# Summing the adaLN vectors of a two-layer backbone on VectorE in place of TensorE

## The chip, the cores and the metric

One core of one Trainium2 chip. The metric is the device time of the whole kernel in microseconds, the median of the runs. TensorE (PE) multiplies, VectorE (DVE) and ScalarE (ACT) do elementwise work, GpSimd (POOL) and SyncE (SP) issue the loads here.

## What is computed

Two streams of 256 tokens, 1024 wide each (context and latent), pass through two layers. Layer 0 mixes with an S5 scan beside four retention heads, layer 1 with mLSTM heads; a squared-ReLU MLP follows each. Before every mixer and every MLP stands an RMS norm with an adaLN shift and scale, and behind every one an adaLN gate. The adaLN vectors are products of two conditioning vectors with a wide weight:

```python
silu_c = jax.nn.silu(c)          # latent stream
silu_cc = jax.nn.silu(c_ctx)     # context stream
for layer in range(DEPTH):       # DEPTH = 2, N_MOD = 6, mod_w[layer] is 1024 x 6144
    ctx_out = layer < DEPTH - 1
    m_lat = [m[:, None, :] for m in jnp.split(silu_c @ mod_w[layer] + mod_b[layer], N_MOD, axis=-1)]
    m_ctx = jnp.split(silu_cc @ mod_w[layer] + mod_b[layer], N_MOD, axis=-1)
    h_lat = modulate(rms_norm(lat, norm_mix_g[layer]), m_lat[0], m_lat[1])
    h_ctx = modulate(rms_norm(cx, norm_mix_g[layer]), m_ctx[0], m_ctx[1])
    ...                          # the mixer of the layer
    lat = lat + m_lat[2] * y_lat
    h2 = modulate(rms_norm(lat, norm_mlp_g[layer]), m_lat[3], m_lat[4])
    lat = lat + m_lat[5] * sq_relu_mlp(h2, mlp_w1[layer], mlp_w2[layer])
    if ctx_out:                  # layer 0 alone: the context stream gets the same
        ...
return rms_norm(lat, final_norm_g)
```

So layer 0 needs all six vectors (c = 0 to 5) for both streams; layer 1 needs c = 0 and 1 for both streams and c = 2 to 5 for the latent stream alone.

## The kernel before, in words

Activations lie with the model width on the partitions (eight tiles of 128 x 512: 256 context tokens, then 256 latent tokens). Every large product is made of three reduced-precision products: the weight tile (128 x 1024) and the activation are each split into a high and a low part, the high part by a cast on ScalarE, the low part by a subtraction on VectorE. A matmul of 128 x 512 with such a part is the common TensorE instruction; each weight tile thus asks for one `CAST w` on ScalarE and one `TENSOR_TENSOR w` on VectorE before its products can be finished.

*Order of the work.* Nothing is written out in order. `body`, `even_mixer`, `mlp` and `odd_mixer` only record operations, each under the name of a group (`chu11` a part of the S5 scan, `head1` two retention heads, `glu`, `wo0` the output projection of layer 0, `nm0` the norm before layer 0's MLP, `mlp00a` the first half of that MLP, `nm` and `gt` the norm and first products of layer 1's mixer). `Plan.order` then places them on five in-order queues (PE, V, A, G for GpSimd, SP) with a list scheduler: its costs, capacities `CAPS` and, for each group, a pair of numbers in `SHIFT` and `AGAIN` (how far the group's due time is moved, and how far ahead it may take a buffer). All instructions are issued in one loop in `Plan.emit`, so each carries one line number, L693 before and L698 after.

*The vectors.* `sc` holds SiLU of both conditioning vectors (columns 0 and 1 of 32; the other 30 are zero). The first two vectors of layer 0 go through `mod_first`, loaded by SP. The other ten go through `mod(l, c, both)`: eight rows of the weight (tiles of 128 x 1024 from `in_modc`, loaded by GpSimd into the buffers `m`, of which there are 2, or `e`, of which there are 5 and which the scan uses too). With `both` (layer 0's c = 2 to 5 and layer 1's c = 0, 1) TensorE adds up each row as it lands, four products of 32 columns side by side (`ps<-m,sc` or `ps<-e,sc`). Without it (layer 1's c = 2 to 5, latent alone) VectorE sums the rows into a tile `e`, scaled per partition (`SCALAR_TENSOR_TENSOR e<-e,sc,e`, the first of eight a `TENSOR_SCALAR`), and TensorE then makes four products of 32 columns with the constant `second` (a column of ones at place 1), which add over the partitions. Either way ScalarE copies the result to `mrow`, TensorE transposes it and VectorE adds the bias into `mc`. For the norm `mod_gain` makes `gm` of it.

*Who needs them when.* Layer 0's c = 2 is read by the residual additions of `wo0`, c = 3 and 4 by `nm0`, c = 5 by the residual additions of the MLP. The norm `nm0` sums squares with products by `ones`, computes the reciprocal root on VectorE in tiles `rs`, spreads it by products with `ident`, and then scales, shifts and splits tile by tile.

Of the kernel before, what the change touches and what calls it, by code (L numbers as in the profile page):

```python
# [21 lines left out]
HORIZON, ROUNDS = 92, 6  # L22
SHIFT = {"": (-41, -100), "chu00": (-8, 8), "chu01": (0, 5), "chu10": (-1, -89), "chu11": (2, 27), "decay0": (-1, 46),
# [16 lines left out]
AGAIN = (  # L40
# [654 lines left out]
def body(tc, I, out, dbg=None):  # L695
    nc = tc.nc
    plan = Plan(CAPS)
# [3 lines left out]
    def const(shape, tag, dt=F32):  # L701
        return plan.buf("@" + tag, shape, dt)
# [64 lines left out]
    gm = [[const((128, 8, 2), f"gm{l}{j}") for j in range(2)] for l in range(2)]  # L767
    sc = const((128, 8, 32), "sc")
    msel = const((128, 2), "msel")
    second = const((128, 32), "second")  # L770

    def stage(src):
        st = wt()
# [1040 lines left out]
```

## Time and profile before

| | |
|---|---|
| median of 3 runs | 1227.14 us (1225.52 to 1228.25) |
| profiled execution | 1225.47 us, its span 1223.7 us |
| granted TensorE clock, mean | 0.978 |
| TensorE, VectorE, ScalarE busy | 96%, 63%, 45% of the span |

A row of the busy time by stage gives the stretch, its length, then busy us and number of instructions (x) for PE, PE's weight load, DVE, ACT and POOL, where they have any, then the granted clock, the share of the DMA engines and GB/s. A row of the timeline gives start, busy time, engine, line, operation, what it writes and reads (numbers of buffers left out), and in brackets how long the engine sat idle before it and what ended that. A row of the chain gives start, length and what it was.

### The profile page before, as it was taken

How to read it: one execution, taken by the hardware profiler on the slowest of the kernel's cores; microseconds unless marked ns; L12 is line 12 of the kernel's file. 1: busy time of each engine (PE TensorE's matmuls, PEld its weight loads, DVE VectorE, ACT ScalarE, POOL GpSimd, SP SyncE). 2: the span in 40 equal slices, each digit the busy share in tenths (PEclk: the TensorE clock that was granted, in tenths of full speed). 3: DMA queues.
4: the chain of work that ended last, by engine and by line, in shares of the span. 5: the costliest groups of instructions: out<-in, count | busy, mean ns of one | idle time of the engine just before them, and what ended most of it. 6: DMA issues, size and time to landing. Idle time of an engine off the chain costs nothing.

```text
span 1223.7 us, 17752 instructions
## 1 busy us (share of the span) xinstructions
PE 1172.9 (96%) x6968; PEld 972.0 (79%) x6968; DVE 770.6 (63%) x1535; ACT 552.8 (45%) x890; POOL 43.2 (4%) x85
## 2 busy tenths in 40 slices
PE   5799999999989999999999999999999998999996
PEld 3577877777758888888787877767888897999996
DVE  8999899464454347434346485956577566765655
ACT  3635535552343332223243146676665444643542
POOL 0001001101020001000000000000000000000000
PEclk9799999999999999999999989999999998999998
DMA  9764225446472337523253532202222253455552
GB/s 353 260 205 132 89 87 160 162 136 226 159 269 95 121 102 233 182 87 124 92 188 138 198 121 86 64 24 69 90 75 87 87 178 136 169 172 190 207 190 70
DMA packets 61923, 177.75 MB, mean 145 GB/s; under 512 B 10768, under 2 KB 17104, under 8 KB 61840
## 3 DMA queue, kind: packets, MB, share of 16 engines
q1 hardware_dynamic: 50320, 134.67, 33.0%
q0 software_dynamic: 11520, 41.95, 10.0%
q8 instruction: 55, 0.90, 0.3%
q14 instruction: 28, 0.23, 0.1%
HBM read 174.01 MB, written 2.59 MB: 144 GB/s over the span
## 4 chain that ended last, share of the span: by engine, by line
PE 64%; issue 16%; DVE 13%; DMA 3%; ACT 3%; POOL 0%; SPq 0%; DVEq 0%; POOLq 0%; ACTq 0%
PE ps L693 64%; DVE b L693 10%; DMA e<-in_modc 2%; DVE w L693 2%; ACT b L693 2%; ACT w L693 1%; DMA dram<-b 1%; DVE e L693 1%; DVE rs L693 0%; DMA vec<-in_vec 0%; ACT L693 0%; DVE sm L693 0%; POOL e L693 0%; DVE pw L693 0%; DVE lgs L693 0%
## 5 line engine op out<-in xcount | busy, mean ns | idle before, releaser
L693 PE MATMUL ps<-b,w 128*128 128x512 f32 (+1 forms) x4920 | 921.3, 346 | 7.6 <-ACT w L693 4.0
L693 PEld LDWEIGHTS ps<-b,w 128*128 128x128 f32 x4920 | 769.6, 190 | 133.8 <-issue 8.8
L693 DVE TENSOR_TENSOR w<-w,w 128x1024 fp32r<-128x1024 f32 x209 | 255.6, 1223 | 225.1 <-PE ps L693 173.5
L693 ACT CAST w<-w 128x1024 fp32r<-128x1024 f32 x209 | 218.5, 1048 | 374.2 <-PE ps L693 165.3
L693 DVE TENSOR_TENSOR b<-b,b 128x512 f32<-128x512 f32 (+4 forms) x276 | 153.1, 574 | 66.8 <-ACT b L693 57.8
L693 PE MATMUL ps<-b,b 128*128 128x256 f32 (+5 forms) x832 | 149.1, 333 | 1.8 <-DMA b<-dram 1.5
L693 PEld LDWEIGHTS ps<-b,b 128*128 128x128 f32 (+1 forms) x832 | 110.9, 183 | 27.1 <-issue 18.2
L693 ACT COPY b<-ps 128x256 f32<-128x256 f32 (+4 forms) x132 | 58.5, 459 | 42.4 <-PE ps L693 30.8
L693 ACT ACTIVATE b<-ps 128x256 f32<-128x256 f32 (+1 forms) x112 | 49.8, 459 | 50.7 <-PE ps L693 48.9
L693 ACT CAST b<-b 128x512 fp32r<-128x512 f32 (+2 forms) x112 | 56.5, 527 | 34.5 <-DVE b L693 31.3
L693 ACT ACTIVATE b<-b 128x256 f32<-128x256 f32 (+2 forms) x75 | 37.4, 513 | 47.6 <-DVE b L693 42.1
L693 DVE SCALAR_TENSOR_TENSOR b<-b,vec,b 128x512 f32<-128x512 f32 (+1 forms) x80 | 53.2, 691 | 8.9 <-ACT b L693 8.3
L693 DVE TENSOR_TENSOR b<-b 128x256 f32<-128x256 f32 (+2 forms) x95 | 43.6, 476 | 15.8 <-ACT b L693 15.7
L693 DVE SCALAR_TENSOR_TENSOR b<-ps,mc,b 128x256 f32<-128x256 f32 x72 | 31.8, 478 | 32.8 <-PE ps L693 32.8
L693 ACT ACT_TABLE_LOAD x36 | 46.2, 1283 | 7.5 <-DMA cc<-in_cc 6.8
L693 POOL DMA_DIRECT2D e<-in_modc x56 | 29.8, 533 | 412.5 <-DVE e L693 238.5
L693 DVE SCALAR_TENSOR_TENSOR e<-e,sc,e 128x1024 f32<-128x1024 f32 x28 | 35.9, 1281 | 5.6 <-DMA e<-in_modc 5.3
L693 DVE SCALAR_TENSOR_TENSOR b<-ps,b 128x512 f32<-128x512 f32 (+1 forms) x32 | 19.3, 620 | 25.2 <-PE ps L693 16.7
L693 PE MATMUL ps<-e,sc 128*32 128x256 f32 x240 | 20.7, 444 | 10.6 <-DVE sc L693 8.6
L693 PEld LDWEIGHTS ps<-w,b 128*128 128x128 f32 x192 | 24.1, 188 | 3.1 <-issue 2.1
L693 PE MATMUL ps<-w,b 128*128 128x256 f32 x192 | 26.1, 287 | 0.0
L693 DVE TENSOR_TENSOR b<-pw,b 128x512 f32<-128x512 f32 x36 | 23.9, 681 | 0.0
(120 smaller groups left out, 525.6 us busy)
## 6 DMA issues: line engine op xcount, KB each, us to landing
w<-in_w SPq DMA_DIRECT2D x128, 512.0 KB, 4.4
e<-in_modc POOLq DMA_DIRECT2D x56, 512.0 KB, 5.1
m<-in_modc POOLq DMA_DIRECT2D x24, 512.0 KB, 4.8
w<-in_evin SPq DMA_DIRECT2D x16, 512.0 KB, 4.5
w<-in_mlx SPq DMA_DIRECT2D x16, 512.0 KB, 3.8
w<-in_mlo SPq DMA_DIRECT2D x16, 512.0 KB, 3.7
w<-in_mlout SPq DMA_DIRECT2D x16, 512.0 KB, 4.1
b<-in_xT SPq DMA_DIRECT2D x16, 256.0 KB, 8.3
```

The source lines that it names most:

```text
L693: o.ins.append(getattr(engine, name)(*[f(a) for a in args], **{k: f(v) for k, v in kw.items()}))
```

## The change

`mod` no longer sums rows on TensorE for any vector. VectorE sums the rows for each stream that is needed, into one tile `e` per stream (two for c = 2 to 5 of layer 0 and c = 0, 1 of layer 1), and TensorE then makes four products of 32 columns per stream with the constant `pick`, whose part s has ones in column s; both streams' products add into one bank. Each vector has a group of its own (`mod02` to `mod15`). The table of offsets is another one, with another `HORIZON`.

```diff
-HORIZON, ROUNDS = 92, 6
+HORIZON, ROUNDS = 70.0, 6
...
-    second = const((128, 32), "second")
+    pick = const((128, 2, 32), "pick")
...
         pr = ps()
-        tag = "m" if (l, c) < (0, 5) else "e"
-        with plan.group(f"mod{l}{'pe' if both else 'dve'}"):
-            acc = None if both else wt(tag="e")
+        streams = (0, 1) if both else (1,)
+        with plan.group(f"mod{l}{c}"):
+            acc = {s: wt(tag="e") for s in streams}
             for k in range(8):
-                st = wt(tag=tag)
+                st = wt(tag="m" if (l, c) < (0, 5) else "e")
                 with plan.group(plan.name + ".s"):
                     G.dma_start(st, I["modc"][6 * l + c - 2, k])
-                if both:
-                    for q in range(4):
-                        PE.matmul(pr[32 * q:32 * q + 32, 0:256], sc[:, k, :], st[:, 256 * q:256 * q + 256], start=k == 0, stop=k == 7)
-                elif k == 0:
-                    ts(acc, st, sc[:, k, 1:2], MUL)
-                else:
-                    stt(acc, st, sc[:, k, 1:2], acc, MUL, ADD)
-            if not both:
+                for s in streams:
+                    if k == 0:
+                        ts(acc[s], st, sc[:, k, s:s + 1], MUL)
+                    else:
+                        stt(acc[s], st, sc[:, k, s:s + 1], acc[s], MUL, ADD)
+            for s in streams:
                 for q in range(4):
-                    PE.matmul(pr[32 * q:32 * q + 32, 0:256], second, acc[:, 256 * q:256 * q + 256], start=True, stop=True)
+                    PE.matmul(pr[32 * q:32 * q + 32, 0:256], pick[:, s], acc[s][:, 256 * q:256 * q + 256],
+                              start=s == streams[0], stop=s == 1)
...
-    V.memset(x.second, 0.0)
-    V.memset(x.second[:, 1:2], 1.0)
+    V.memset(x.pick, 0.0)
+    for s in range(2):
+        V.memset(x.pick[:, s, s:s + 1], 1.0)
```

What the new order does is seen at two places. In its rows a buffer's name carries two numbers, the second its place in the order of making. The first place is TensorE's queue between the last product of `wo0` and the first of `mlp00a`. Before (its last twelve rows; `rs` is the reciprocal root, `mrow` a vector on its way into `mc`, the last two rows are the MLP's):

```order
L693 MATMUL ps_702_3314<-e_703_3320,sc_65 32x256 x4
L693 MATMUL ps_453_1989<-m_705_3333,sc_65 32x256 x4
L693 MATMUL ps_702_3314<-e_707_3347,sc_65 32x256 x4
L693 MATMUL ps_716_3399<-ident_73,rs_713_3377 128x128 x4
L693 MATMUL ps_453_1989<-m_708_3352,sc_65 32x256 x4
L693 MATMUL ps_702_3314<-e_711_3369,sc_65 32x256 x4
L693 MATMUL ps_453_1989<-ident_73,mrow_719_3416 128x128 x2
L693 MATMUL ps_702_3314<-e_712_3371,sc_65 32x256 x4
L693 MATMUL ps_702_3314<-e_714_3381,sc_65 32x256 x4
L693 MATMUL ps_702_3314<-e_715_3392,sc_65 32x256 x4
L693 MATMUL ps_732_3462<-b_727_3449,w_679_3177 128x512
L693 MATMUL ps_732_3462<-b_727_3449,w_681_3197 128x512
```

And now, from `wo0`'s last product:

```order
L698 MATMUL ps_646_2933<-b_641_2909,w_662_3062 128x512
L698 MATMUL ps_691_3229<-ones_97,b_658_3045 128x1
L698 MATMUL ps_691_3229<-ones_97,b_666_3083 128x1
L698 MATMUL ps_691_3229<-ones_97,b_658_3045 128x1
L698 MATMUL ps_691_3229<-ones_97,b_666_3083 128x1
L698 MATMUL ps_691_3229<-ones_97,b_658_3045 128x1
L698 MATMUL ps_691_3229<-ones_97,b_666_3083 128x1
L698 MATMUL ps_691_3229<-ones_97,b_658_3045 128x1
L698 MATMUL ps_691_3229<-ones_97,b_666_3083 128x1
L698 MATMUL ps_693_3248<-ident_155,rs_692_3238 128x128 x4
L698 MATMUL ps_700_3269<-b_695_3256,w_673_3130 128x512
L698 MATMUL ps_700_3269<-b_695_3256,w_676_3154 128x512
```

The steps with `sc` are gone from there, and only the norm's own products stand between projection and MLP.

The second place is VectorE's queue where the GLU ends and `wo0` begins. Before (rows with `vec` are the GLU's, `w` are low parts of weights, rows with `mc` are `wo0`'s residual additions with c = 2):

```order
L693 SCALAR_TENSOR_TENSOR b_640_2957<-ps_628_2906,vec_77,b_629_2914 128x8x64
L693 TENSOR_TENSOR b_644_2977<-b_640_2957,b_642_2965 128x512
L693 TENSOR_TENSOR w_658_3044<-w_619_2866,w_630_2925 128x1024
L693 TENSOR_TENSOR w_659_3046<-w_622_2872,w_638_2953 128x1024
L693 SCALAR_TENSOR_TENSOR b_645_2979<-ps_652_2993,mc_56_255,b_645_2979 128x256 x2
L693 TENSOR_TENSOR w_664_3082<-w_631_2927,w_661_3053 128x1024
```

And now (the sums of c = 4, one row of the weight for both streams each two lines):

```order
L698 SCALAR_TENSOR_TENSOR e_543_2480<-m_627_2851,sc_89,e_543_2480 128x1024
L698 SCALAR_TENSOR_TENSOR e_580_2643<-m_627_2851,sc_89,e_580_2643 128x1024
L698 SCALAR_TENSOR_TENSOR e_543_2480<-m_644_2921,sc_89,e_543_2480 128x1024
L698 SCALAR_TENSOR_TENSOR e_580_2643<-m_644_2921,sc_89,e_580_2643 128x1024
L698 SCALAR_TENSOR_TENSOR e_543_2480<-m_647_2941,sc_89,e_543_2480 128x1024
L698 SCALAR_TENSOR_TENSOR e_580_2643<-m_647_2941,sc_89,e_580_2643 128x1024
L698 SCALAR_TENSOR_TENSOR e_543_2480<-m_649_2960,sc_89,e_543_2480 128x1024
L698 SCALAR_TENSOR_TENSOR e_580_2643<-m_649_2960,sc_89,e_580_2643 128x1024
L698 SCALAR_TENSOR_TENSOR e_543_2480<-m_650_2978,sc_89,e_543_2480 128x1024
L698 SCALAR_TENSOR_TENSOR e_580_2643<-m_650_2978,sc_89,e_580_2643 128x1024
L698 TENSOR_TENSOR w_652_3010<-w_626_2841,w_640_2904 128x1024
L698 TENSOR_TENSOR w_654_3021<-w_502_2329,w_559_2545 128x1024
```

Ten sums have come in ahead of the two weight splits that stood there. In all, the 48 sums of c = 2, 3 and 4 have come onto VectorE ahead of `nm0`, beside the same other work as before. The sums of c = 3 and 4 of layer 1 have moved from before the norm `nm` to behind it, into layer 1's mixer.

More of the change, by code (lines that the diff above doesn't have):

```diff
@@ L21 @@
 CAPS = {"b": 59, "w": 10, "e": 5, "m": 2, "ps": 8, "mrow": 2, "rs": 3, "tz": 2, "mv": 2, "mv1": 2, "den": 2}
-HORIZON, ROUNDS = 92, 6
-SHIFT = {"": (-41, -100), "chu00": (-8, 8), "chu01": (0, 5), "chu10": (-1, -89), "chu11": (2, 27), "decay0": (-1, 46),
[16 rows of a table removed]
-AGAIN = (
[20 rows of a table removed]
+HORIZON, ROUNDS = 70.0, 6
+SHIFT = {"": (-36, 109), "chu00": (-51, 3), "chu01": (0, 156), "chu10": (0, -53), "chu11": (2, 27), "decay": (1, -71),
[19 rows of a table added]
+AGAIN = (
[5 rows of a table added]
+         (25.8, 220), "gat1.w": (99.4, 400), "glu": (-13.5, -16), "glu.w": (0, 280), "gt": (-16.2, 106), "gt.w":
[16 rows of a table added]
 )
@@ L821, in mod @@
                 PE.transpose(pr[:, 256 + 128 * j:384 + 128 * j], row[:, 128 * j:128 * j + 128], ident)
-            s0 = 0 if both else 1
+            s0 = streams[0]
             b = vc("modb", 48 * l + 8 * c, 8).rearrange("p (q j) -> p q j", j=2)
```

76 rows, old and new, of tables (AGAIN, SHIFT) are left out of this document.

## The prediction

> **What bounds the kernel now.** I read the page first (busy shares and the forty slices), then busy time by stage, then the chain of waits, and at the places it names the timeline. On the page, these rows show who is busy when; a slice is 30.6 us.
>
> ```profile
> PE 1172.9 (96%) x6968; PEld 972.0 (79%) x6968; DVE 770.6 (63%) x1535; ACT 552.8 (45%) x890; POOL 43.2 (4%) x85
> ...
> PE   5799999999989999999999999999999998999996
> DVE  8999899464454347434346485956577566765655
> ...
> PEclk9799999999999999999999989999999998999998
> ```
>
> TensorE looks busy throughout, but VectorE is full in the first seven slices. The busy time by stage (busy us and instructions of PE, weight load, DVE, ACT, POOL; then clock and DMA) separates the two:
>
> ```profile
> 0.00:210.00 210.00, 183.85 (x1263) 144.00 (x1264) 195.46 (x542) 100.25 (x192) 12.37 (x27) 0.95 0.54 185
> 10.00:210.00 200.00, 182.77 (x1255) 143.80 (x1256) 191.23 (x510) 97.11 (x187) 10.90 (x21) 0.95 0.53 182
> 120.00:150.00 30.00, 28.92 (x222) 23.98 (x222) 24.37 (x70) 15.92 (x32) 0.53 (x1) 0.94 0.37 116
> 210.00:340.00 130.00, 128.56 (x720) 97.42 (x718) 63.61 (x112) 57.18 (x89) 9.16 (x18) 1.00 0.51 171
> 0.00:348.00 348.00, 318.62 (x2056) 244.99 (x2056) 263.03 (x660) 159.38 (x284) 25.75 (x52) 0.97 0.54 182
> 340.00:358.00 18.00, 14.23 (x156) 7.05 (x152) 11.00 (x30) 4.66 (x10) 6.86 (x13) 0.91 0.98 350
> 358.00:720.00 362.00, 362.00 (x1589) 292.27 (x1588) 177.21 (x236) 115.07 (x162) 14.84 (x28) 1.00 0.43 145
> 720.00:778.00 58.00, 53.67 (x233) 41.14 (x232) 40.99 (x89) 38.11 (x61) 0.00 (x0) 0.91 0.14 46
> ```
>
> Until 210 us VectorE sets the pace: after the first 10 us it is busy 191.23 of 200 (95.6%). From 210 to 340 TensorE does (128.56 of 130), with VectorE half idle (63.61). Then comes a hole from 340 to 358, where both wait and the DMA engines are full (0.98). From 358 to 720, layer 0's MLP, TensorE has no idle time at all, so there every TensorE instruction added or removed counts.
>
> The hole, in the chain of waits (first row) and the timeline of all engines (the rest):
>
> ```profile
> 340.41 5.21 DMA e<-in_modc
> ...
> 338.55 0.96 PE L693 MATMUL ps<-b,w 128*128 128x512 f32 x3
> ...
> 345.67 0.64 PE L693 MATMUL ps<-e,sc 128*32 128x256 f32 x8 [0.81 <-DMA e<-in_modc]
> ...
> 348.22 0.16 DVE L693 TENSOR_SCALAR rs<-ps 128x4 f32<-128x4 f32 x1 [3.08 <-PE ps L693]
> ...
> 354.78 0.17 DVE L693 TENSOR_TENSOR mc<-ps,vec 128x16 f32<-128x16 f32 x1
> ...
> 357.60 2.70 PE L693 MATMUL ps<-b,w 128*128 128x512 f32 x10 [0.74 <-ACT b L693]
> ```
>
> The last product of layer 0's output projection ends at 339.5; the MLP's first stands at 357.6, 18.1 us later. Between them TensorE sums adaLN vectors row by row as the rows land, and `mc`, the MLP's scale, is written only at 354.78. The same boundary one layer on, where no vector needed for the norm waits for rows:
>
> ```profile
> 720.22 0.64 PE L693 MATMUL ps<-e,second 128*32 128x256 f32 x8
> ...
> 722.77 0.16 DVE L693 TENSOR_SCALAR rs<-ps 128x4 f32<-128x4 f32 x1
> ...
> 728.25 1.22 PE L693 MATMUL ps<-b,w 128*128 128x512 f32 x2 [1.51 <-ACT b L693]
> ```
>
> It takes 8.0 us from 720.2, of which 5.5 lie behind the first `rs`.
>
> **Part 1: what leaves and enters TensorE.** Six vectors times eight rows are 48 steps of four products (8 instructions in the trace). Busy time of these alone, in four stretches, and of the pair products that four vectors use already:
>
> ```profile
> 0.00:66.00 66.00, 16.48 (x152) 5.14 (x152) 0.45 (x2) 0.22 (x1) 0.87 0.77 286
> 66.00:210.00 144.00, 9.99 (x128) 3.21 (x128) 0.00 (x0) 0.00 (x0) 0.99 0.43 138
> 210.00:340.00 130.00, 7.83 (x112) 2.72 (x112) 0.00 (x0) 0.00 (x0) 1.00 0.51 171
> 340.00:358.00 18.00, 9.71 (x124) 3.05 (x120) 0.00 (x0) 0.00 (x0) 0.91 0.98 350
> 600.00:730.00 130.00, 2.56 (x32) 0.63 (x32) 0.00 (x0) 0.98 0.45 156
> ```
>
> The first row holds 128 instructions of the first two vectors, which stay, so 24/8 = 3 steps go there, 16 before 210, 14 before 340 and 15 in the hole: 48. One step costs 7.83/14 = 0.56 us beside other work. The 19 before 210 lie where VectorE sets the pace: worth nothing. Twelve more products of the kept kind are added: six before the MLP, six after it, in stretches where TensorE is full. The six after cost 6 x 0.56 = 3.4 us (bounds: 6 x 0.64 = 3.8 by the last row, and 0 if they fall into waits). **+3.4.**
>
> **Part 2: what enters VectorE.** Rows of the sums it does today (by tile; the third from the timeline, four in a row):
>
> ```profile
> L693 DVE SCALAR_TENSOR_TENSOR e<-e,sc,e x28: 1273/1282/1286, 465.7 to 714.4; 128x1024 f32<-128x1024 f32 x28
> L693 DVE TENSOR_SCALAR e<-e,sc x4: 746/750/753, 453.9 to 674.7; 128x1024 f32<-128x1024 f32 x4
> 471.35 5.24 DVE L693 SCALAR_TENSOR_TENSOR e<-e,sc,e 128x1024 f32<-128x1024 f32 x4
> ```
>
> One stream of one vector is 0.75 + 7 x 1.28 = 9.7 us, both 19.45. Three vectors (c = 2, 3, 4) have to be there before or at the MLP's norm: +58.4 us. The other three (6 streams, another 58.4) stand in the MLP, where VectorE is busy 177.21 of 362: hidden by TensorE, and if that cover went they would cost their length.
>
> VectorE did 263.0 us up to the norm's first `rs` at 348.2; now 263.0 + 58.4 = 321.4 must be done before the same point, since otherwise the same instructions stand before it. Of these 195.5 are done by 210, leaving 125.9 where 67.6 stood. TensorE up to there falls from 318.6 by 9.99 + 7.83 and some, so VectorE becomes the longer of the two. If it stays as full as from 10 to 210 (95.6%), 125.9 takes 131.7 and `rs` comes at 341.7; the order leaves nothing but the norm itself behind it on TensorE, so the MLP starts 5.5 later: 347.2.
>
> Against that stands the place in VectorE's order where ten sums of c = 4 follow each other (five rows) ahead of two weight splits of the output projection. The rows pass through two tiles `m`, and a tile is refilled only after both its sums:
>
> ```profile
> DMA to landing us min/median/max: 3.7/4.9/12.0
> DMA to landing us min/median/max: 3.8/4.5/7.5
> ```
>
> (The first is all loads of these rows, the second those from 450 to 510, where VectorE did such sums.) Two rows take 2.56 + 4.9 = 7.5, so 3.7 each against 2.56 of work: 1.2 lost per row, 6 for five. TensorE has the GLU's products to do meanwhile, so I take half, 3.0, between 0 and 6. The MLP then starts at 350.2 and not at 357.6: **-7.4.** Bounds of this term: VectorE without any idle time and no row waits, 210 + 125.9 + 5.5 = 341.4 (-16.2); and as full as from 120 to 150, its worst stretch while it set the pace (24.37 of 30, 81%), with 6 of row waits, 210 + 155 + 11.5 = 376.5 (+18.9). I take the first value since it is the mean over 200 us of the same kind of work.
>
> **Part 3: the rest.** The sums of two one-stream vectors (c = 3, 4 of layer 1) move behind layer 1's norm, 19.4 us into a stretch where VectorE is busy 40.99 of 58 and TensorE 53.67: the 17 idle hold one of them, if waits there leave room. Bounds 0 and 9.7 (one vector all in the way); I take 1.0, nearer the idle row. **+1.0.** The row loads are the same 80 on POOL's queue. The first 210 us are written in another order too (more of the scan ahead of the heads); I cost it at nothing as long as VectorE stays as full there as now, and a percent less would cost 2.
>
> Sum: -7.4 + 3.4 + 1.0 = -3.0. The profiled execution took 1225.5 (span 1223.7), which gives 1222.5; the median of the runs lies 1.7 above it, so 1224.
>
> **A rule against it.** `TENSOR_SCALAR` takes 750 ns where the two-operand form takes 1282 for as many elements. The Trainium skill, SBUF — State Buffer, section SBUF: two separate sides, says that a VectorE operation in a two-port mode (which such a faster form points to) locks GpSimd out, so that loads issued by GpSimd starve for descriptors; all 80 row loads are issued there. In the trace, loads beside such sums landed in a median 4.5, no later than all of them at 4.9, which does not bear it out.
>
> **The rivals.**
> - *TensorE stays the bound* (0.17). VectorE's sums all fit into its idle time. Then 14 x 0.56 = 7.8 of steps go and 3.4 of products come between 210 and 340, and the hole shrinks from 18.1 to 8.0: -14.5, with +3.4 and +0 behind it -11: 1216, and less if the 16 steps before 210 (9.99) count too: 1206. For it: 85 us of VectorE idle before 348 (348 - 263). Against: 14.5 of them lie before 210.
> - *VectorE becomes the bound and loses time* (0.27), the case on the other side. It works in order, and between 210 and the norm it must wait for products of the heads, for casts and for rows, while weight splits for TensorE queue behind the sums. The change turns to a loss when the MLP starts after 357.6 - 4.4 = 353.2, so `rs` with 3.0 of row waits by 344.7: 125.9 of 134.7, a share of 93.5%. Below it the kernel is slower; at 87%, half way to the worst stretch, the MLP starts at 363.2: +5.6 + 4.4, 1237; at 81% 1247. For it: no stretch before asked both engines for so much.
> - *The wait only changes its owner* (0.18): rows and sums end as late as TensorE's steps did, MLP at about 354: 1227.
> - *Row loads starve behind VectorE* (0.05), the case of the rule above: at the longest landing seen, 12.0, a row takes (2.56 + 12.0)/2 = 7.3, five rows lose 23.6 in place of 3.0: 1245.
>
> **The numbers.** The forecast has 0.33. About 0.2% (2.5 us) is what a measurement of this kernel can tell from no change. Of the forecast 0.28 is faster by more, with 0.17 from the first rival: 0.45. Same: 0.05 of the forecast and the third rival, 0.23. Slower: 0.27 + 0.05 = 0.32. The forecast's own range is 1218 to 1228; the whole, between the first rival's two values and the second's, with about 0.1 left out at each end, 1208 to 1243.
>
> **What would show it.** Right: the hole before the MLP near 8 us without row steps; first MLP product near 350; VectorE busy over 93% from 210 to there; row waits of some 3 us before the ten sums of c = 4; MLP stretch longer by 3. Wrong: MLP start after 353 with TensorE waiting for `w` splits in the GLU or output projection; a granted clock under 1.00 between 210 and 340; row loads landing later than 6 us; layer 1's mixer longer by over 3.

## The result: slower by 1.0%, and the profile after

The changed kernel takes 1239.43 us (median of 4 runs, 1236.22 to 1241.21) against 1226.33 of the kernel before beside it (1225.47 to 1228.25): a ratio of 1.0102, 95% interval 1.0076 to 1.0127. I had forecast 1224. The profiled execution took 1240.03, its span 1238.2; before it was 1225.47 and 1223.7.

The page after, the rows that were shown of before (a slice is now 31.0 us):

```profile
PE 1162.5 (94%) x6680; PEld 975.0 (79%) x6680; DVE 876.8 (71%) x1632; ACT 552.5 (45%) x887; POOL 43.3 (3%) x85
PE   3899989899979999999999989999999997999996
DVE  8999899899764764666845467986557766755564
PEclk9899899999979999999999989899999998999998
```

TensorE has lost 10 us of work and VectorE has gained 106, as the change says. VectorE's full stretch now reaches to the tenth slice, where it was seven before. The busy time by stage:

```profile
0.00:210.00 210.00, 174.90 (x1184) 145.97 (x1185) 195.34 (x519) 112.18 (x203) 2.52 (x8) 0.94 0.43 147
210.00:340.00 130.00, 122.57 (x560) 92.08 (x559) 113.74 (x178) 47.02 (x77) 12.71 (x24) 0.99 0.50 166
210.00:353.00 143.00, 131.78 (x600) 99.80 (x598) 120.82 (x193) 50.89 (x82) 12.71 (x24) 0.97 0.49 166
345.70:358.30 12.60, 5.64 (x25) 5.32 (x25) 6.33 (x19) 2.63 (x6) 0.00 (x0) 0.59 0.16 60
358.30:724.00 365.70, 365.07 (x1614) 293.62 (x1615) 216.34 (x272) 119.22 (x166) 20.66 (x39) 1.00 0.47 156
724.00:734.50 10.50, 6.52 (x54) 5.22 (x52) 7.24 (x22) 5.12 (x10) 1.06 (x2) 0.80 0.34 120
```

Until 210 us VectorE does what it did (195.34, before 195.46). From 210 to 353, where the norm's first `rs` comes, it works 120.82 of 143, a share of 84%. The hole ahead of layer 0's MLP (345.7 to 358.3) is 12.6 us long with the clock at 0.59.

Cut at TensorE's first product of layer 0's MLP, of layer 1's mixer and of layer 1's MLP, the two traces give:

| stretch | before | after | difference |
|---|---|---|---|
| start to layer 0's MLP | 357.6 | 358.3 | +0.7 |
| layer 0's MLP, to the mixer's first product | 370.6 | 376.2 | +5.6 |
| layer 1's mixer, to its MLP's first product | 298.6 | 306.7 | +8.1 |
| the rest | 196.9 | 197.0 | +0.1 |

So nothing was gained ahead of the MLP, where I had put 7.4, and two stretches that I had put at 3.4 and 1.0 cost 13.7. How exact is one such trace? Up to the end of the output projection the changed kernel and four kernels below (`a_no1314`, `a_back`, `a_back2`, `a_warm`) issue the same instructions; their profiled executions reached it at 345.7, 343.6, 347.2, 346.2 and 343.9. A stage is good to about 2 us on either side, and I read smaller differences only where a row names their cause.

*Ahead of the MLP.* VectorE's waits between 210 and 353 (total, times, longest), one of its row waits, the norm's first row on VectorE, and TensorE's queue around the hole:

```profile
DVE e L698 <- DMA m<-in_modc: 7.6, 7, 3.5
DVE w L698 <- PE ps L698: 4.1, 4, 2.3
DVE rs L698 <- PE ps L698: 3.7, 1, 3.7
DVE b L698 <- ACT b L698: 3.6, 5, 1.2
DVE b L698 <- PE ps L698: 2.0, 1, 2.0
```

```profile
233.90 1.28 DVE L698 SCALAR_TENSOR_TENSOR e<-m,sc,e 128x1024 f32<-128x1024 f32 x1 [3.48 <-DMA m<-in_modc]
352.80 0.16 DVE L698 TENSOR_SCALAR rs<-ps 128x4 f32<-128x4 f32 x1 [3.73 <-PE ps L698]
```

Then TensorE:

```profile
344.71 0.95 PE L698 MATMUL ps<-b,w 128*128 128x512 f32 x3
349.22 3.55 PE L698 MATMUL ps<-ones,b 128*128 128x1 f32 x16 [3.56 <-DVE b L698]
354.69 2.05 PE L698 MATMUL ps<-ident,rs 128*128 128x128 f32 x8 [1.93 <-DVE rs L698]
358.25 8.07 PE L698 MATMUL ps<-b,w 128*128 128x512 f32 x27 [1.51 <-ACT b L698]
```

VectorE waits most for weight rows. From 210 us to the end of the output projection TensorE now waits 7.3 us in all, 1.4 before. The longest of these waits, 3.76 us at 235.8, is for a result of VectorE and stands right behind the row wait shown, so there the wait for a row went on to TensorE. In the hole TensorE first waits 3.56 us for the last residual sum; then 16 products by `ones` take 3.55 us, and those by `ident` 2.05. In the hole of the kernel before, between its row steps, the same products took 1.95 and 1.44:

```profile
346.24 1.95 PE L693 MATMUL ps<-ones,b 128*128 128x1 f32 x16
350.91 1.44 PE L693 MATMUL ps<-ident,rs 128*128 128x128 f32 x8
```

*In the MLP.* TensorE's instructions from the MLP's first product to its last, by form (count, busy us, mean ns, idle time before them), in the kernel before:

```profile
L693 PE MATMUL ps<-b,w 128*128 128x512 f32 x1536 | 358.6, 395 | 0.7 <-ACT b L693 0.7
L693 PE MATMUL ps<-b,b 128*128 128x128 f32 x19 | 2.6, 275 | 0.0
L693 PE MATMUL ps<-e,second 128*32 128x256 f32 x16 | 1.3, 391 | 0.0
```

And after:

```profile
L698 PE MATMUL ps<-b,w 128*128 128x512 f32 x1536 | 360.3, 396 | 2.1 <-ACT b L698 1.5 <-DVE w L698 0.6
L698 PE MATMUL ps<-b,b 128*128 128x128 f32 x26 | 3.5, 274 | 0.0
L698 PE MATMUL ps<-e,pick 128*32 128x256 f32 x48 | 3.2, 385 | 0.0
```

The new products cost 1.9 (3.2 - 1.3: those for six streams came, and those of two vectors of layer 1 left), products that came here from the boundary 0.9, and 1536 unchanged products 1.7 more. Most of those 1.7 lie at the start, where the clock is low: 10 products stand in the first 3.7 us, where the pace of before gives 15. The first stretch before:

```profile
357.60:362.00 4.40, 4.40 (x18) 3.41 (x19) 4.26 (x10) 4.40 (x10) 0.12 (x1) 1.00 0.78 298
```

And after, at 0.55:

```profile
358.30:362.00 3.70, 3.70 (x10) 2.79 (x11) 3.70 (x9) 3.64 (x8) 0.00 (x0) 0.55 0.00 0
```

*In the mixer.* Its first 58 us before:

```profile
728.20:786.20 58.00, 55.67 (x216) 42.70 (x217) 43.40 (x89) 38.58 (x60) 0.00 (x0) 0.92 0.19 61
```

And after, where VectorE has 5.3 us more to do and TensorE is busy 1.5 us less:

```profile
734.50:792.50 58.00, 54.16 (x229) 42.67 (x229) 48.72 (x97) 36.57 (x58) 4.76 (x9) 0.89 0.52 167
```

Not all of the mixer's 8.1 us can lie with the moved sums. At its end, ahead of the next norm's products, TensorE now waits 4.0 us for VectorE, 2.2 before; it does so in `a_no1314` of part 4 too, which leaves these sums out.

The rival that rows starve behind VectorE is out: in the page's list of loads they land in a median 4.1 and 4.5 us (4.9 for all of them before).

```profile
e<-in_modc POOLq DMA_DIRECT2D x56, 512.0 KB, 4.5
m<-in_modc POOLq DMA_DIRECT2D x24, 512.0 KB, 4.1
```

The rule that I weighed there (the Trainium skill, SBUF — State Buffer, section SBUF: two separate sides) is thus not borne out by this trace either. It is hardly tested by it: only 16 of the 128 sums have the faster form (0.75 us) that the rule was weighed for.

### The profile page after: what moved, and what is told of

The parts are those of the page before. It is cut to its first block, busy times and chain, and to the rows that moved or that the text cites. A ratio compares the mean times of both kernels' runs of the same rounds, so it can differ in the third digit from the quotient of the medians.

```text
span 1238.2 us, 17257 instructions
## 1 busy us (share of the span) xinstructions
PE 1162.5 (94%) x6680; PEld 975.0 (79%) x6680; DVE 876.8 (71%) x1632; ACT 552.5 (45%) x887; POOL 43.3 (3%) x85
## 4 chain that ended last, share of the span: by engine, by line
PE 70%; DVE 11%; issue 9%; DMA 4%; ACT 2%; DVEq 0%; POOL 0%; SPq 0%; POOLq 0%; ACTq 0%
PE ps L698 70%; DVE b L698 7%; DVE e L698 3%; DMA m<-in_modc 2%; DMA e<-in_modc 1%; DVE w L698 1%; DMA w<-in_mlx 1%; ACT b L698 1%; ACT w L698 1%; DVE rs L698 1%; ACT L698 0%; DVE sm L698 0%; DVE den L698 0%; DVE mc L698 0%; POOL b L698 0%
## 5 line engine op out<-in xcount | busy, mean ns | idle before, releaser
L698 PE MATMUL ps<-b,b 128*128 128x256 f32 (+5 forms) x832 | 155.1, 344 | 7.7 <-DVE b L698 5.5
L698 PEld LDWEIGHTS ps<-b,b 128*128 128x128 f32 (+1 forms) x832 | 114.0, 190 | 33.5 <-issue 14.8
L698 DVE SCALAR_TENSOR_TENSOR e<-e,sc,e 128x1024 f32<-128x1024 f32 x70 | 88.0, 1280 | 26.2 <-DMA e<-in_modc 25.9
L698 DVE SCALAR_TENSOR_TENSOR e<-m,sc,e 128x1024 f32<-128x1024 f32 x42 | 52.4, 1278 | 7.7 <-DMA m<-in_modc 7.6
L698 PE MATMUL ps<-ones,b 128*128 128x1 f32 x112 | 17.7, 281 | 23.8 <-DVE b L698 23.8
L698 PEld LDWEIGHTS ps<-ones,b 128*128 128x128 f32 x112 | 17.9, 241 | 25.8 <-DVE b L698 20.2
```

Of the source, the lines that this page charges most:

```text
L698: o.ins.append(getattr(engine, name)(*[f(a) for a in args], **{k: f(v) for k, v in kw.items()}))
```

## Experiments

Sixteen kernels. All keep the order of their parent (the kernel before, names `b_`, or the changed one, `a_`) and edit it after the scheduler has run, so that one thing moves at a time; a new plan would have rearranged the whole program. The ratios are against the kernel before on the same chip, whose median there lay between 1225.97 and 1227.87.

### 1. The sums ahead of the norm

Rows 2 to 8 of each vector are summed by 7 instructions for each stream. `a_own234` gives the 42 of layer 0's c = 2, 3 and 4 the running sum in place of the loaded row, `a_no234` leaves them out, `a_no6` leaves out 84 (also c = 5 of layer 0 and c = 0, 1 of layer 1, which stand in the MLP).

```diff
 stt(acc[s], st, sc[:, k, s:s + 1], acc[s], MUL, ADD)
+# a_no234: not emitted if (l, c) in ((0, 2), (0, 3), (0, 4)); a_no6: six vectors
+# a_own234: for these, emitted as stt(acc[s], acc[s], sc[:, k, s:s + 1], acc[s], MUL, ADD)
```

> The changed kernel in its order, where the same 42 sums read their own running sum in place of the row: same instructions and lengths, but no wait for a row. If the row waits (7.6 us on VectorE, of it 3.5 in a row of ten sums just ahead of the output projection's weight splits) are passed on to TensorE: MLP start 3 to 7 earlier, 1233 to 1237. If VectorE's work itself sets the pace and the waits fall into time in which it would wait for TensorE anyway: under 2 us, 1238 to 1240.

> The changed kernel in its order, with the 42 sums of rows 2 to 8 of layer 0's c = 2, 3, 4 left out (the vectors are then made of the first row alone); rows are still loaded, products and everything else stay. If VectorE's sums ahead of the MLP hold TensorE up (it waits 12.9 us in all between 210 and 358, VectorE is 84% busy there): the MLP starts 8 to 14 us earlier than at 358.3 and the kernel takes 1225 to 1232. If the new order itself is at fault there (the sums fill idle time): no more than the 7.6 us of row waits go, and those only if they lie on the path: MLP start after 354, kernel 1235 to 1240.

> As the first of these, with the sums of layer 0's c = 5 and layer 1's c = 0 and 1 left out too (84 in all). If sums hidden behind the MLP's products cost nothing: MLP stretch as in the changed kernel, 376 from its first product to the mixer's, and the same time as the first of these. If VectorE's 39 us more there delay weight splits or evictions: the stretch shortens by 2 to 4 (it was 370.6 before the change, and six more products are about 3.4 of the 5.6).

| | time (runs) | ratio, 95% | MLP starts | MLP stretch | mixer |
|---|---|---|---|---|---|
| `a_own234` | 1229.03 (10) | 1.0007, 0.9991 to 1.0024 | 350.7 | 376.0 | 301.1 |
| `a_no234` | 1227.34 (10) | 1.0005, 0.9988 to 1.0022 | 346.0 | 378.7 | 303.9 |
| `a_no6` | 1226.87 (10) | 0.9995, 0.9978 to 1.0012 | 345.8 | 376.4 | 303.6 |

TensorE's first product of the MLP in `a_own234`, and in a second view its hole (both end at 350.7):

```profile
350.68 1.65 PE L700 MATMUL ps<-b,w 128*128 128x512 f32 x3 [1.51 <-ACT b L700]
```

```profile
338.10:350.70 12.60, 5.60 (x26) 5.28 (x25) 6.34 (x19) 2.65 (x5) 0.00 (x0) 0.60 0.15 60
```

The same product in `a_no234`:

```profile
346.00 1.22 PE L700 MATMUL ps<-b,w 128*128 128x512 f32 x2 [1.51 <-ACT b L700]
```

Without row waits the MLP starts 7.6 us earlier, as much as VectorE had waited for rows, and TensorE's waits from 210 us to the end of the projection fall from 7.3 to 2.0. The time fell by more, 0.95% or some 11.6 us: in this trace the mixer is 5.6 us shorter too, which the edit does not touch and no run here explains. That is a larger gain than either expectation held. With the sums themselves left out the MLP starts another 4.7 earlier, but the time is the same (ratios 1.0007 and 1.0005), so that their own work costs anything is not shown. The hole is 12.6 us in `a_own234` and 11.7 in `a_no234`. 42 more sums left out inside the MLP change nothing in the time, and the stretch is 376.4, against 376.2 in the changed kernel and 378.7 in `a_no234`: where the change put those, they are hidden, as far as 2 us can tell. And even with 42 of the 48 sums ahead of the norm left out the changed order only reaches the time of before. Its MLP starts 11.6 us earlier than before (346.0 for 357.6), and the MLP and the mixer lose all of it again (8.1 and 5.3).

### 2. TensorE's steps, and what makes the hole before

`b_nosteps` leaves out of the kernel before the middle six of each vector's eight steps on TensorE, rows still loaded. `b_no1` leaves out 12 of the 16 rows of layer 1's c = 0 and 1, with their loads: they are needed 360 us later, but stand around the hole.

```diff
 PE.matmul(pr[32 * q:32 * q + 32, 0:256], sc[:, k, :], st[:, 256 * q:256 * q + 256], start=k == 0, stop=k == 7)
+# b_nosteps: not emitted for 0 < k < 7
+# b_no1: for (l, c) in ((1, 0), (1, 1)) and 0 < k < 7 neither this nor the row's load
```

> The kernel before in its order, with the 36 middle steps of TensorE's 48 left out (rows 2 to 7 of eight; the vectors are made of two rows). It bounds what taking the steps off TensorE can give when nothing is put in their place. If a step costs 0.56 us where TensorE is full and the hole before the MLP is made by the steps and their rows: 10 or 11 steps of 0.56 between 210 and 340, and the hole of 18.1 us shrinks by 4 to 8: 1212 to 1217. If the steps lie in waits anyway: 1223 to 1227.

> The kernel before, in its order, with 12 of the 16 rows of layer 1's c = 0 and 1 left out, their loads and their TensorE steps (the first and the last of each vector stay). These rows are not needed before layer 1, but stand on POOL's and TensorE's queues around the hole ahead of layer 0's MLP. Theory 'the hole of before is made by loading rows': with them gone the hole shrinks from 18.1 us to 10 to 14, the MLP starts 4 to 8 earlier, and the time falls to 1218 to 1223. Rival 'the hole is made by the norm's own chain and by c = 4': hole 16 to 18, time 1225 to 1229.

`b_nosteps` took 1227.65 (10 runs), ratio 0.9997 (0.9978 to 1.0016); `b_no1` 1224.21 (10 runs), ratio 0.9979 (0.9959 to 0.9998). TensorE's queue in the hole of `b_nosteps`:

```profile
347.26 3.54 PE L695 MATMUL ps<-ones,b 128*128 128x1 f32 x16 [1.57 <-DVE mc L695]
352.72 2.04 PE L695 MATMUL ps<-ident,rs 128*128 128x128 f32 x8 [1.93 <-DVE rs L695]
...
360.03 1.22 PE L695 MATMUL ps<-b,w 128*128 128x512 f32 x2 [2.00 <-ACT b L695]
```

36 steps at 0.56 us, 20 us of TensorE work, are worth nothing. The hole stays 18.0 us (342.0 to 360.0), and where the steps are gone from it the granted clock falls (0.63 for 0.90 over the hole) and the norm's own products take 3.54 and 2.04 for 1.95 and 1.44. So the steps were filling in a wait, not making it. Without the next layer's loads the hole is 16.4 and the kernel 0.2% faster: by the hole they cost 1.7 us there.

### 3. One part of the change alone

`b_dve1` is the kernel before with layer 1's c = 0 and 1 summed on VectorE in the first 90 us of layer 0's MLP, by the changed kernel's instructions. `b_dve1e` also loads c = 4's last four rows 40 us earlier, into the tiles `e` that this frees, and has their steps within the output projection.

```diff
-(l, c) in ((1, 0), (1, 1)): 16 row loads, 16 steps and the two biases around the hole
+the same loads, 32 sums and 16 products by a column of ones, behind the norm
+b_dve1e: rows 5 to 8 of (0, 4) in tiles e, load and step some 50 places earlier in the order
```

> The kernel before with one part of the change alone, put where VectorE has room: layer 1's c = 0 and 1 for both streams are loaded and summed on VectorE behind layer 0's norm, in the MLP (32 sums, 16 products of 32 columns), every other instruction in its old place. Theory 'the hole is made by loading rows': the MLP starts 4 to 8 us earlier, its stretch grows by 1 to 3 (products and a few late splits), time 1220 to 1224. Rival 'VectorE's sums cost wherever they stand' (splits queue behind them in the MLP, too): the stretch grows by 6 or more, time 1226 to 1231.

> As the version before (layer 1's c = 0 and 1 on VectorE in layer 0's MLP), and the last four rows of layer 0's c = 4 are loaded some 40 us earlier into the tiles e that became free, with their TensorE steps and the vector's bias inside the output projection instead of behind it. Theory 'the hole is made by loading rows': hole 8 to 10 as at layer 1's boundary, time 1217 to 1221. Rival 'the steps cost as much inside the projection as they free behind it' (6 x 0.56 = 3.4 us): no more than 2 us below the version before, 1222 to 1225 if that one gains.

Both were slower: `b_dve1` 1234.01 (10 runs), ratio 1.0051 (1.0032 to 1.0069); `b_dve1e` 1237.64 (5 runs), ratio 1.0078 (1.0051 to 1.0106). The MLP of `b_dve1` starts at 356.1 but takes 379.7 (370.6 before). TensorE's only wait within it, from the timeline:

```profile
385.92 12.96 PE L715 MATMUL ps<-b,w 128*128 128x512 f32 x48 [3.36 <-ACT w L715]
```

That wait is 3.4 of the 9.1 us; behind it 48 products take 270 ns each, where 1536 took 233 in the kernel before. The hole of `b_dve1e` in stretches (the first without any TensorE instruction; the last is the MLP's start) and what ends that wait:

```profile
342.00:347.00 5.00, 0.00 (x0) 0.00 (x0) 4.07 (x6) 1.57 (x2) 0.00 (x0) 0.73 0.00 0
347.00:351.00 4.00, 3.55 (x16) 3.49 (x16) 0.23 (x3) 0.00 (x0) 0.00 (x0) 0.50 0.00 0
359.20:363.00 3.80, 3.80 (x8) 2.63 (x9) 3.76 (x11) 3.14 (x7) 0.53 (x1) 0.50 0.00 0
```

```profile
347.16 3.55 PE L724 MATMUL ps<-ones,b 128*128 128x1 f32 x16 [5.25 <-DVE b L724]
```

The end of the hole, with what VectorE does ahead of the MLP's first product:

```profile
354.71 3.08 DVE L724 TENSOR_TENSOR b<-b,ps 128x512 f32<-128x512 f32 x5 [2.23 <-PE ps L724]
359.18 5.40 PE L724 MATMUL ps<-b,w 128*128 128x512 f32 x11 [4.50 <-ACT b L724]
```

In `b_dve1e` no row is loaded in the hole any more, and it is still 17.3 us long (341.9 to 359.2). My theory of loading rows fell here. The hole is the norm's own chain: the last residual sums on VectorE (5.25 us), products by `ones`, `rs`, products by `ident`, scaling and splitting. Emptied of row steps, that chain runs at half clock, and so do the MLP's next 4 us. Its length hangs on the order of VectorE's work, too. In the changed kernel the products by `ones` and `ident` take as long (3.55 and 2.05), but its hole is 4.7 us shorter: TensorE waits 3.56 us and not 5.25 for the last residual sum, and 1.51 and not 4.50 behind the products by `ident`, since VectorE there begins with the scaling of one tile (0.87 us) and does not multiply five tiles first (3.08 us). So the shorter hole came with the new order, not with the steps that left it. The rival of `b_dve1` held, with more than its 1226 to 1231: sums that VectorE does ahead of weight splits hold them up (3.36 us for a weight whose cast came late; the cast had waited 2.36 us for a split on VectorE that came after two sums), though `a_no6` showed the same kind of sums free at other places.

### 4. The sums that moved into the mixer

`a_no1314` leaves out 14 sums (rows 2 to 8 of layer 1's c = 3 and 4). `a_back` and `a_back2` do the whole work and put these two vectors back into layer 0's MLP: `a_back` both in a row in its last third with two or three row tiles; `a_back2` c = 3 early, with four tiles, and c = 4 in the last 35 us.

```diff
+# a_no1314: sums not emitted if (l, c) in ((1, 3), (1, 4))
+# a_back: loads and sums of (1, 3), (1, 4) at places 2009 to 2129 of the order (were 2234 to 2559)
+# a_back2: (1, 3) at 1636 to 1678, (1, 4) at 2136 to 2206
```

> The changed kernel's order with 14 sums left out: rows 2 to 8 of c = 3 and 4 of layer 1, the two one-stream vectors that the change moved behind layer 1's norm (their rows are still loaded, the tile keeps the first row's product). Layer 1's mixer, from its first product to the last MLP's first, took 298.6 us before and 306.7 after. Theory 'the moved sums are in the way': the mixer falls back to 298 to 301 and the time to 1231 to 1234. Rival 'the rest of the order is slower there' (VectorE's share is low, the weight loads or splits stand otherwise): the mixer stays at 303 to 307 and the time at 1237 to 1241.

> The changed kernel with one part of the change undone: the sums of c = 3 and 4 of layer 1 (and their loads) stand again in layer 0's MLP, where VectorE works on little in the last 35 us, and not in layer 1's mixer; c = 5's sums of layer 1 move a little later for it, and c = 2's four products come earlier into the MLP. All other instructions keep their places. Theory 'the moved sums are in the mixer's way' (leaving them out gave 6 to 7 us): the mixer falls from 306.7 to 298 to 302 us, the MLP grows by 0 to 2, time 1231 to 1235. Rival 'sums cost the same wherever they stand, since splits queue behind them': the MLP grows by 4 or more, time 1237 to 1241.

> The changed kernel with the sums of c = 3 and 4 of layer 1 in layer 0's MLP once more, this time where VectorE's queue is thin and tiles are free: c = 3 between c = 5 of layer 0 and c = 0 of layer 1 with four row tiles, c = 4 in the MLP's last 35 us with two tiles and 4 us per row; all else in its place. Theory 'what hurt in the first attempt were row waits ahead of weight splits, not the sums': TensorE waits in the MLP for no more than 3 us, its stretch grows by 0 to 2 over 376, the mixer is 298 to 301, time 1232 to 1236. Rival 'VectorE's sums cost in the MLP, too': the stretch grows by 4 or more, time 1237 to 1243.

| | time (runs) | ratio, 95% | MLP stretch | mixer |
|---|---|---|---|---|
| `a_no1314` | 1234.30 (10) | 1.0046, 1.0026 to 1.0067 | 378.1 | 299.2 |
| `a_back` | 1245.79 (4) | 1.0137, 1.0115 to 1.0160 | 389.1 | 299.3 |
| `a_back2` | 1236.03 (6) | 1.0071, 1.0053 to 1.0089 | 380.9 | 297.2 |

The first 58 us of the mixer in `a_no1314`, with TensorE busy throughout:

```profile
734.30:792.30 58.00, 58.00 (x264) 46.66 (x265) 46.13 (x102) 41.11 (x66) 6.29 (x12) 0.96 0.59 209
```

TensorE's longest wait in `a_back`'s MLP, and VectorE's waits for rows from 600 to 748 us:

```profile
663.27 16.30 PE L743 MATMUL ps<-b,w 128*128 128x512 f32 x59 [5.37 <-ACT w L743]
```

```profile
DVE e L743 <- DMA e<-in_modc: 15.1, 11, 3.6
```

The latter in `a_back2`, from 600 to 739 us:

```profile
DVE e L742 <- DMA e<-in_modc: 10.7, 9, 5.0
```

All three agree on the mixer: 297 to 299 us without these sums. Over all kernels made from the changed one that have them there it takes 301.1 to 306.7 (six traces, mean 304.0), without them 296.7 to 300.6 (six, mean 298.7): 5.3 us. Putting them back has its own price, which differs by place: 13 us in `a_back`, 5 in `a_back2`. In `a_back` VectorE waited 15.1 us for rows, and the trace shows one such wait go on to TensorE: a row wait of 3.59 us at 659.7, behind it a weight split, then the cast that TensorE waited 5.37 us for. In `a_back2` VectorE waited 10.7 us for rows, but TensorE's longest wait in the MLP is 0.80; of the 5 us some 2 lie at the boundary to the mixer, where TensorE waits 2.57 us for VectorE (0.51 in the changed kernel), and the rest is open. In both the stretch grew by more than the 2 us that I had expected at most, and the time of `a_back` lies even above its rival's 1237 to 1241.

### 5. Row tiles, clock, and all together

`a_rows` gives the rows of c = 3 and 4 more tiles. `a_warm` adds 21 products of `ident` with itself in the hole. `a_all` joins `a_rows`, `a_warm`, `a_back` and a shorter end of the residual sum; `a_best` the same with `a_back2` and more fillers in the later norms; `a_sum` takes the three costs away from the changed kernel and does less work than it. `b_warm` is the kernel before with fillers in the gaps of its norms.

```diff
+# a_rows: 10 rows of (0, 3), (0, 4) in turn in tiles m, m, e, e, e; three loads of (0, 5) later
+# a_warm: 12, 5, 4 times PE.matmul(dump[:, 0:128], ident, ident, start=True, stop=True)
+#         behind wo0's last product, the norm's products by ones, those by ident
+# b_warm: the same call, 7 times in nm0, 13 in nm, 17 in nm1, 6 in the final norm
```

> The changed kernel with more tiles for the rows: the rows of c = 3 and 4 of layer 0 from 250 us on go in turn through the two tiles m and, from 250, one tile e and, from 300, two more, which stood idle or held rows of c = 5 long before their sums; c = 5's first three loads come later. The order of all sums is kept. Theory 'the run of c = 4 waits for its rows' (3.5 us of waits in that run, up to 4 more of them elsewhere; reading the sum instead of the row gave 7.6): the MLP starts 3 to 5 us earlier than 358.3, time 1234 to 1237. Rival 'the wait goes to the next in line' (VectorE then waits for products or casts): MLP start within 1.5 of 358, time 1238 to 1241.

> The changed kernel with 21 more TensorE products, of ident with itself into a free bank, which nobody reads: 12 behind the output projection's last product, 5 behind the norm's products by ones, 4 behind those that spread the reciprocal root. Theory 'the row steps in the hole of before were free and kept the clock up' (granted clock in the hole and the 4 us behind it 0.50 to 0.77 after, 0.76 to 1.00 before; the products by ones take 3.55 for 1.95, those by ident 2.05 for 1.44): the clock stays near 1.00 there, the MLP starts 1.5 to 2.5 earlier and its first stretch is 1 to 2 shorter, time 1235 to 1237. Rival 'the hole is VectorE's chain alone': MLP start within 0.7 of 358.3, time 1238 to 1242, the fillers merely lying in the wait.

> The changed kernel with the three mends together (layer 1's sums back in the MLP, more tiles for the rows, fillers in the hole), and at the end of the output projection one weight split set behind the last residual sum and one sum ahead of it. Theory 'three causes that add' (7 + 4 + 3 and 1 to 2 for the tail): 1222 to 1227, as fast as before or a little faster. Rival 'they cover the same wait': no better than the best of the three alone, 1231 to 1236.

> The changed kernel's order with the three costs taken away at once: rows 2 to 8 of c = 2, 3 and 4 of layer 0 are summed from the running sum itself and not from the loaded row (so they wait for no row; the rows are still loaded), the same rows of c = 3 and 4 of layer 1 are left out (14 sums), and the 21 fillers stand in the hole ahead of layer 0's MLP. Theory 'row waits (7.6), sums in the mixer (7), cold clock (4) add up to more than the whole loss of 13': 1220 to 1224, faster than before. Rival 'they cover one another': 1226 to 1230, as each of the first two reached with others left in.

> The kernel before, in its order, with 43 fillers on TensorE (products of ident with itself into a free bank, read by nobody), in the gaps of the norms: 7 in the hole ahead of layer 0's MLP, 13 ahead of layer 1's mixer, 17 ahead of layer 1's MLP, 6 in the final norm. In these gaps the granted clock falls to 0.50 to 0.62 and stays at 0.50 to 0.53 for the next 4 us of products. Theory 'a gap costs twice, by its length and by the clock behind it': 1.5 to 3 us less at each of the two boundaries of layer 1 and 0.5 at the others, 1219 to 1224. Rival 'the clock behind a gap is set by the wait itself, and fillers only come on top': 1226 to 1230.

> The changed kernel with all mends: layer 1's sums in the MLP at those places, more row tiles for c = 3 and 4 of layer 0, the tail of the residual sum in a shorter order, fillers in the hole ahead of layer 0's MLP and in the gaps of the later norms. Theory 'the costs are separate': MLP start 353, MLP stretch 374, mixer 299, so 1221 to 1226, level with the kernel before or a little faster. Rival 'VectorE's sums cost where they stand': 1229 or more.

| | time (runs) | ratio, 95% | MLP starts | MLP stretch | mixer |
|---|---|---|---|---|---|
| `a_rows` | 1237.06 (7) | 1.0066, 1.0047 to 1.0086 | 356.2 | 376.4 | 306.1 |
| `a_warm` | 1233.63 (10) | 1.0046, 1.0028 to 1.0064 | 354.8 | 374.3 | 302.7 |
| `a_all` | 1238.18 (4) | 1.0079, 1.0058 to 1.0100 | 353.0 | 385.9 | 299.1 |
| `a_sum` | 1219.78 (6) | 0.9942, 0.9922 to 0.9962 | 349.2 | 375.0 | 300.6 |
| `b_warm` | 1224.50 (12) | 0.9985, 0.9968 to 1.0003 | 367.6 | 370.8 | 296.1 |
| `a_best` | 1225.50 (12) | 0.9995, 0.9979 to 1.0011 | 352.0 | 375.5 | 296.7 |

(`b_warm`'s profiled execution took 1232.4, far from its median; its 367.6 is that execution's.) VectorE's wait for rows that is left in `a_rows` between 210 and 351:

```profile
DVE e L732 <- DMA m<-in_modc: 3.5, 1, 3.5
```

The hole of `a_warm` on TensorE, and the MLP's first 3.7 us by stage:

```profile
343.74 2.84 PE L728 MATMUL ps<-ident 128*128 128x128 f32 x24
347.36 1.95 PE L728 MATMUL ps<-ones,b 128*128 128x1 f32 x16 [0.79 <-DVE b L728]
```

```profile
354.80:358.50 3.70, 3.65 (x16) 2.86 (x17) 3.70 (x10) 3.64 (x8) 0.00 (x0) 0.99 0.00 0
```

The first 4 us of the mixer before:

```profile
728.20:732.20 4.00, 3.96 (x9) 2.98 (x10) 4.00 (x12) 3.89 (x8) 0.00 (x0) 0.50 0.01 4
```

And in `b_warm`:

```profile
738.40:742.40 4.00, 3.80 (x15) 2.83 (x16) 4.00 (x12) 3.89 (x8) 0.00 (x0) 1.00 0.00 0
```

With fillers the products by `ones` take 1.95 again, the hole is 10.9 and not 12.6, and the MLP's first 3.7 us hold 16 products for 10. That is 1.7 us in the hole and 1.9 in the MLP's stretch, 3.6 by the trace; the time fell by 0.56% of 1226, some 7, and I can't name the rest: the trace shows 1.8 less ahead of the hole and 4.0 less in the mixer, which the fillers don't touch and which is about the scatter of traces. The direction is shown, the size of the clock's part is 3.6 to 7. `a_rows` took 4.1 of the 7.6 us of row waits away and gave some 2 (356.2 for 358.3); the wait that it left is the one of 233.9 us, the one that went on to TensorE whole. Its interval overlaps that of the changed kernel, so its gain is not shown. `a_all`, of which I had expected 1222 to 1227, keeps the gain ahead of the MLP (353.0) and loses it in the MLP (385.9), which it has from `a_back`.

`a_sum` answers whether the costs add: it is 1.6% below the changed kernel, 19.6 us of 1226, where row waits (0.95%), sums in the mixer (0.56%) and clock (0.56%) come singly to 2.1%, or 25. Whether they have anything in common is not shown: the changed kernel's own interval, 0.25% to either side, enters that sum three times. `a_best`, which does the whole work, mends the loss to a tie with the kernel before (1225.50 against 1226.29). No version here that does the whole work is shown to beat the kernel before; `b_warm` comes nearest, but its interval holds 1, and 0.15% is less than the 1.5 to 3 us that I had expected at each of two boundaries. Ahead of layer 0's MLP its fillers had nothing to win: the clock behind that hole was 1.00 before.

## Why the prediction was wrong, step by step

The step that failed first is VectorE's share of 95.6% in part 2, and with it the -7.4; the second is the +1.0 of part 3. The traces are 14.5 us apart, where my sum had -3.0. Of the 17.5 between, 8.1 lie in the MLP's start, 7.1 in the mixer and 2.2 in the MLP.

- **TensorE's steps were not the price of the hole (part 1, first rival).** A step does take 0.56 us, but `b_nosteps` shows 36 of them worth nothing. I read the hole as made by row steps and late rows; by `b_no1` and `b_dve1e` it is a chain of the norm, into which the steps and loads fitted, and the steps kept the clock up in it. The hole did shrink, to 12.6 and not to 8, but by the new order of VectorE's work (part 3 of the experiments), since without row steps in the old order it is 17.3.
- **VectorE's share (part 2).** I took 95.6% from the first 200 us, where it waits for little. It was 84%. To `rs` I counted 125.9 of work, 5.8 of idle and 3.0 of row waits; it was 120.8 of work and 22 of idle, of which 7.6 for rows and 13.8 for TensorE, ScalarE and casts. So `rs` came at 352.8 and not 344.7, and the MLP started at 358.3 and not 350.2. The 5.5 us from `rs` to the MLP came true (5.45).
- **Row waits were mis-sized.** The run of ten sums waited 3.5 us. I had counted 6 for it and taken half, since TensorE "has the GLU's products to do meanwhile"; `a_rows`, which took these waits away and gained 2, does not speak against the half. What I had left out is one row far from that run, at 233.9 us, which made VectorE wait 3.48 and TensorE 3.76 behind it; 0.6 more came elsewhere. By `a_own234` the MLP starts 7.6 earlier without any of them.
- **The MLP's +3.4 was +5.6.** The products were 1.9, not 3.4. Low clock, mostly at its start (1.7), products that came in from the boundary (0.9) and a boundary 0.9 longer (10.5 for 9.6) were not in my sum. That the sums there are hidden was right for this order (`a_no6`) and wrong as a rule (`b_dve1`, `a_back`).
- **The mixer's +1.0 was +8.1**, of which the moved sums are 5 to 7 by the traces and `a_no1314`. I took the value near the idle row, "the 17 idle hold one of them". My upper bound of 9.7 held; idle time of an in-order engine was not room. The longer wait at the mixer's end (4.0 for 2.2) was in no term of mine.
- **The rivals.** VectorE as the bound that loses time, at 0.27, had the direction, and its sign that decides (MLP after 353.2) was met. That its price came out near (between 1237 at 87% and 1247 at 81%) is luck: I had it all in the MLP's start, and there it was only +0.7, since the hole itself shrank from 18.1 to 12.6 while the output projection ended 6 us later (345.7 for 339.5). Ahead of the MLP the third rival, the wait that only changes its owner, came nearer, though its 1227 had none of the price behind. Of the signs that I named for a failure three came: MLP after 353, a granted clock under 1.00 between 210 and 340 (by a hair, 0.99), mixer longer by over 3. TensorE did not wait for weight splits there, and rows did not land late, which I had also named.

## What to carry to other kernels

An engine's idle time in a profile is room only if nothing in its in-order queue has to wait: price work moved onto it by the waits that come with it (here 7.6 us for rows in two tiles; a stretch longer by 13 us where they stood ahead of weight splits), not by its duration alone. Before crediting work that leaves a gap, ask what the gap is made of; if it is a chain on other engines, the work was free and may have kept TensorE's clock up. A moved instruction costs where it lands: here two vectors taken out of a stretch of 362 us in which VectorE was half idle, into one of 58 that was nearly full, cost 5 to 7 of the 13 us lost.

## What the hardware showed that I had not expected

A wait of TensorE cost twice here. Behind the 3.56 us wait ahead of the norm's products the granted clock was 0.50 and products by `ones` took 3.55 for 1.95 us; behind the hole, and behind the next boundary of the kernel before, the first 4 us of matmuls held 10 or 9, and with cheap products in the gap 16 or 15 at a clock of 0.99 or 1.00. The Trainium skill, TensorE: Matmul & The Clock Gate, section What's actually happening, gives half clock after an idle window of about 3.4 us and full clock after a busy one. The rows agree with the two values, but not with the length of an idle time: at layer 1's boundary of the kernel before the clock was 0.50 from 724.0 to 725.5 and products by `ident` took 2.04 us, though in the 6 us ahead TensorE had stood idle no longer than 0.53 us, between small products; here the rows count. And executions of the same instructions can differ by 3.6 us over the first 345 (343.6 to 347.2), more than several of the effects that I had tried to add up.
